# Memory-key reads, residual loads and the last rounds of the down product in a decoder layer on Trainium2

## The chip, the cores and the metric

The kernel runs on one core of one Trainium2 chip. The metric is the device time of one execution in microseconds. The kernel before was timed three times: 1323.92, 1323.97 and 1324.94 us, so its median is 1323.97 us.

## The reference

One layer with three residual sub-layers and a final norm, on 1024 tokens of width 1024, all in fp32. What matters here:

```python
def gla_mixer(...):                     # 4 heads, chunks of 64; per-head norm, gain, gate
    ...
    o = o * lax.rsqrt(jnp.mean(o * o, axis=-1, keepdims=True) + EPS) * gla_gain.astype(f32)
    o = o.reshape(B, T, GLA_VW) * jax.nn.silu(r.astype(f32))

def cross_attn(h, memn, w_q, w_k, w_v, w_o):
    k = (memn @ w_k).reshape(B, MEM_LEN, CROSS_HEADS, CROSS_DH)      # 256 memory tokens
    v = (memn @ w_v).reshape(B, MEM_LEN, CROSS_HEADS, CROSS_DH)
    ...

def conv_ffn(h, w_up, conv_w, conv_b, w_down):                       # D_FF = 2816
    ...
    return (jax.nn.silu(gate) * val) @ w_down

h = x
h = h + jnp.concatenate([o_gla, o_swa], axis=-1) @ w_out[l]
h = h + cross_attn(rms_norm(h, norm_cross[l]), rms_norm(mem, norm_mem[l]), ...)
h = h + conv_ffn(rms_norm(h, norm_ffn[l]), w_up[l], conv_w[l], conv_b[l], w_down[l])
return rms_norm(h, norm_final)
```

`rms_norm(x, g)` is `x * rsqrt(mean(x*x) + EPS) * g` along the row of 1024.

## The kernel before

**Arithmetic.** Every fp32 operand of a large product is split into a high part (a cast on ScalarE, L109) and a low part (a subtraction on VectorE, L110); TensorE then does three matmuls for one product, high by high, high by low and low by high (`mm3`, L148 to L150; in the down stage L1405). Where one engine's queue is spoken of: PE is TensorE, DVE is VectorE, ACT is ScalarE, POOL is GpSimd, SP is SyncE. Instructions run in order on each engine, and a DMA is issued by the engine whose queue it is on.

**Stages.** Input projections; sliding-window attention; gated linear attention (`gla`); the output projection with its residual (`mix_out`); cross attention; the up projection; the down projection (`ffn_down`) with the final norm. The products of the memory tokens with w_v_c (parts 0 to 7) and w_k_c (parts 8 to 15) are strewn into `gla` as filler for TensorE (`memory_parts`). In `gla`, DVE and ACT run in the order in which the code is written; elsewhere a scheduler sets the order from the readiness and the place in the program of each instruction, and "issue after" ties add an order without a semaphore of their own where both stand on one engine.

**Memory keys.** For parts 8 to 15 `multiply(n)` does 24 matmuls of 256 columns into one of two PSUM banks with the role O; `read(n)` takes the bank out: high part on ACT (L362), low part on DVE (L365), then a DMA on the POOL queue to `k_d` (L368). The SBUF target is half of a tile `la`, which two parts share (2 such tiles). A bank is free for `parts(n + 2)` when `read(n)` is done. `gla_scaled` (L921) scales the chunk outputs on ACT, 8 instructions, with the factors of `gla_norm`, which end at L190 on DVE.

**mix_out** has 8 steps of 2 halves, each 24 matmuls of 512 columns; the half's evacuation adds the residual (L1103, DVE) in a tile `res` with 3 buffers. `res` is loaded from `xt_d` on the SP queue (L1078), and written to `h1_d` on the POOL queue (L1081). The weights' split for its first step is tied to come after the transposes that precede it.

**ffn_down** (L1378 ff) multiplies 1024 x 2816 by 2816 x 1024 as 2 x 2 blocks in seven products by Winograd's form of Strassen's rule. Each product has 11 steps k, each of 4 banks, 3 matmuls of 512 columns in each bank: 132 matmuls. Operands of a step are sums of blocks (`comb`, L1391, DVE) or blocks as loaded, and are split into `w` slots: 6 slots are 3 pairs, and pairs are made 2 steps ahead (`AHEAD`). The blocks are summed in place, so the sum b12 - b11 overwrites b11. `snapshot` (L1440) adds a product's banks to the residual; `half_row` (L1445) finishes half a row block and has ACT sum its squares (L196) into `acc`; `gain` (L1450) multiplies by the final norm's gain. `row_factors` gives the rsqrt of the rows' mean squares: the two halves are added (L1458), scaled (L182), Ln and Exp on ACT (L183, L184), and one Newton step of four small DVE operations (L187 to L190). `finish` scales the two halves of a row (ACT L1465, DVE L1468) and issues the output DMAs on the SP and ACT queues. In the seventh product the last 3 steps run bank by bank (`tail=3`), so that banks end one after another; row blocks 0 and 1 share their factors, 2 and 3 have their own.

Of the kernel before, what the change touches and what calls it, by code (L numbers as in the profile page):

```python
# [27 lines left out]
P = 128  # L28
T = 1024
D = 1024  # L30
# [30 lines left out]
class Layer:  # L61
# [282 lines left out]
    def memory_parts(self, new):  # L344
# [42 lines left out]
        def multiply(n):  # L387
# [14 lines left out]
            else:  # L402
# [315 lines left out]
    def gla(self, new, prepare, multiply):  # L718
# [37 lines left out]
        with self.tc.manual_schedule(engines={mybir.EngineType.DVE, mybir.EngineType.Activation}):  # L756
# [63 lines left out]
            newton()  # L820
            o = self.gla_scaled(po, r, new)
            read(13)
# [237 lines left out]
    def mix_out(self, new, hcnew):  # L1060
# [6 lines left out]
        for j in range(NK):  # L1067
# [14 lines left out]
            with self.tc.issue_after(self.turned.ins):  # L1082
# [295 lines left out]
    def ffn_down(self, pre, hcnew):  # L1378
# [9 lines left out]
        acc = self.small("facc", [P, NT, 2], bufs=1)  # L1388

# [9 lines left out]
        def product(ps, left, right, first, before=(), later=(), ops=(), tail=1):  # L1399


# [19 lines left out]
            for k in range(n):  # L1421
# [13 lines left out]
                later = later[cut:]  # L1435

# [15 lines left out]
        def row_factors(t, count):  # L1452

            ssq, r = self.small("fssq", [P, 4])[:, :count], self.small("frs", [P, 4])[:, :count]
            guess, newton = self.rsqrt_steps(r, ssq, D, count)

            def first():
                tt(out=ssq, in0=acc[:, t:t + count, 0], in1=acc[:, t:t + count, 1], op=add)  # L1458
                guess()
            return r, [first, newton]  # L1460

        def finish(t, r, done, dc, todo, tc):

            def f():
                nc.scalar.mul(out=done, in_=done, mul=r)  # L1465
                nc.sync.dma_start(out=self.out[0, t * P:(t + 1) * P, 512 * dc:512 * dc + 512], in_=done)
                sl = slice(512 * tc, 512 * tc + 512)
# [214 lines left out]
```

## Time and profile before

| | us |
|---|---|
| median of 3 runs | 1323.97 |
| profiled execution | 1327.92 |
| its span on the core | 1326.2 |
| TensorE busy | 1304.6 (98% of the span) |
| VectorE busy | 917.9 (69%) |
| ScalarE busy | 588.0 (44%) |
| GpSimd busy | 86.5 (7%) |

The profile is one execution, 3.95 us above the median; 1.72 us of it lie outside the span. TensorE's busy time includes modelled ends of its pipelined matmuls, so consecutive matmuls overlap in the timeline: the distance from one start to the next is what a matmul costs. A timeline row with a count stands for several instructions in a row that are printed together. The bracket behind a row is the idle time of its engine before it, and the instruction whose end came last among those it waited for. A granted clock of 1.00 is TensorE at 2.4 GHz, 0.50 is 1.2 GHz.

### The profile page before, as it was taken

What the parts mean: (1) busy time and instruction counts of PE and PEld (TensorE: products, weight loads), DVE (VectorE), ACT (ScalarE), POOL (GpSimd) and SP (SyncE); (2) the same over time, 40 slices, a digit from 0 to 9 for tenths busy, and PEclk for the clock granted to TensorE, in tenths of its full rate; (3) what the DMA queues carried; (4) which work ended last, traced back from release to release, by engine and by line L of the source; (5) the groups of instructions that cost most, each with busy time, mean ns of one, the idle gap of its engine ahead of it and who ended that gap; (6) DMA issues with size and microseconds to landing.
All of it is one profiled execution on the core that took longest, in us unless ns stands there. A gap on an engine that the chain in (4) does not pass through costs nothing.

```text
span 1326.2 us, 17248 instructions
## 1 busy us (share of the span) xinstructions
PE 1304.6 (98%) x6575; PEld 1081.6 (82%) x6575; DVE 917.9 (69%) x1564; ACT 588.0 (44%) x1041; POOL 86.5 (7%) x150
## 2 busy tenths in 40 slices
PE   8999999999999999999999999999999999999997
PEld 8887777989788888888888888888888888788785
DVE  6939763377444433464469998888888887998766
ACT  6525545345433333463344544443444444454454
POOL 1400111102100000001100000000000000000000
PEclk9999999999999999999999999999999999999998
DMA  7632112259544311143212343222222238710203
GB/s 221 186 110 64 61 56 61 64 169 295 173 158 143 112 64 48 32 167 95 81 56 64 124 137 106 80 96 83 76 81 95 80 109 320 253 64 8 72 21 146
DMA packets 141528, 146.89 MB, mean 111 GB/s; under 512 B 15825, under 2 KB 108166, under 8 KB 141446
## 3 DMA queue, kind: packets, MB, share of 16 engines
q1 hardware_dynamic: 129974, 111.02, 26.9%
q0 software_dynamic: 10304, 32.68, 7.0%
q10 hardware_dynamic: 1168, 2.10, 0.4%
q8 instruction: 51, 0.84, 0.3%
q14 instruction: 31, 0.25, 0.1%
HBM read 109.06 MB, written 38.28 MB: 111 GB/s over the span
## 4 chain that ended last, share of the span: by engine, by line
PE 51%; issue 39%; DVE 4%; DMA 2%; POOL 2%; ACT 1%; SPq 0%; POOLq 0%; DVEq 0%; ACTq 0%
PE psF L148 10%; PE psF L149 9%; PE psF L150 9%; PE psF L1405 4%; PE psS L1405 4%; PE psT L1405 2%; PE psO L1405 2%; PE psO L148 1%; PE psO L149 1%; PE psO L150 1%; DVE w L110 1%; PE psO L1037 1%; PE psS L984 1%; PE psS L1024 1%; POOL g_d L1338 1%
## 5 line engine op out<-in xcount | busy, mean ns | idle before, releaser
L109 ACT CAST w<-st 128x1024 fp32r<-128x1024 f32 (+1 forms) x146 | 125.8, 863 | 276.1 <-PE psF L149 102.7
L110 DVE TENSOR_TENSOR w<-st,w 128x1024 fp32r<-128x1024 f32 (+1 forms) x146 | 144.0, 986 | 74.6 <-ACT w L109 73.9
L1327 DVE SCALAR_TENSOR_TENSOR uy<-uy,vec,uy 128x1023 f32<-128x1023 f32 (+1 forms) x88 | 111.9, 1277 | 0.9 <-ACT uy L1325 0.4
L1405 PE MATMUL psF<-w,w 128*128 128x512 f32 x330 | 93.0, 390 | 0.1
L1405 PE MATMUL psS<-w,w 128*128 128x512 f32 x330 | 92.5, 390 | 0.0
L1298 PE MATMUL psS<-a,w 128*128 128x512 f32 x360 | 86.5, 389 | 0.0
L148 PE MATMUL psF<-xh,w 128*128 128x512 f32 x208 | 83.3, 400 | 0.0
L150 PE MATMUL psF<-xh,w 128*128 128x512 f32 x208 | 81.5, 392 | 0.0
L149 PE MATMUL psF<-xl,w 128*128 128x512 f32 x208 | 81.2, 390 | 0.0
L1298 PEld LDWEIGHTS psS<-a,w 128*128 128x128 f32 x360 | 67.6, 188 | 14.0
L1298 PE MATMUL psF<-a,w 128*128 128x512 f32 x324 | 77.8, 389 | 0.0
L1405 PEld LDWEIGHTS psF<-w,w 128*128 128x128 f32 x330 | 61.8, 188 | 13.9 <-DVE w L110 0.8
L1405 PEld LDWEIGHTS psS<-w,w 128*128 128x128 f32 x330 | 62.0, 188 | 12.9
L1298 PEld LDWEIGHTS psF<-a,w 128*128 128x128 f32 x324 | 60.8, 188 | 12.6
L148 PE MATMUL psF<-act,w 128*128 128x512 f32 x176 | 69.5, 395 | 0.0
L149 PE MATMUL psF<-act,w 128*128 128x512 f32 x176 | 69.1, 392 | 0.0
L150 PE MATMUL psF<-act,w 128*128 128x512 f32 x176 | 68.8, 391 | 0.0
L1325 ACT ACTIVATE uy<-uy,vec 128x1024 f32<-128x1024 f32 x44 | 54.8, 1246 | 24.8 <-DVE uy L1318 16.9
L1298 PE MATMUL psS<-act,w 128*128 128x512 f32 x240 | 57.8, 389 | 0.0
L1298 PE MATMUL psS<-act,wx 128*128 128x512 f32 x240 | 57.6, 389 | 0.0
L1298 PEld LDWEIGHTS psS<-act,wx 128*128 128x128 f32 x240 | 45.1, 188 | 9.3
L1298 PEld LDWEIGHTS psS<-act,w 128*128 128x128 f32 x240 | 45.1, 188 | 9.3
(396 smaller groups left out, 3041.2 us busy)
## 6 DMA issues: line engine op xcount, KB each, us to landing
st<-in_w_up_dram SPq DMA_DIRECT2D x44, 512.0 KB, 4.0
g_d<-uy POOLq DMA_DIRECT2D x22, 512.0 KB, 2.9
act<-in_w_down_dram SPq DMA_DIRECT2D x12, 512.0 KB, 9.9
st<-g_d SPq DMA_DIRECT2D x10, 512.0 KB, 3.9
res<-g_d SPq DMA_DIRECT2D x10, 512.0 KB, 8.7
st<-in_w_in_dram SPq DMA_DIRECT2D x9, 512.0 KB, 6.6
xt_d<-pts POOLq DMA_DIRECT2D x16, 256.0 KB, 5.4
ow_d<-pts POOLq DMA_DIRECT2D x32, 128.0 KB, 3.1
```

What stands on the lines that cost most here:

```text
L109: h = nc.scalar.copy(out=hi, in_=src)
L110: l = nc.vector.tensor_tensor(out=lo, in0=src, in1=hi.bitcast(F32), op=ALU.subtract)
L148: mm(out, lhsT=lh, rhs=rh, start=start, stop=False)
L149: mm(out, lhsT=lh, rhs=rl, start=False, stop=False)
L150: mm(out, lhsT=ll, rhs=rh, start=False, stop=stop)
L984: nc.tensor.matmul(ps[u][g][:, t, :nk], lhsT=self.sq[2 * u + t][pr, q], rhs=self.sk[pr, k0:k0 + nk], start=True, stop=True)
L1024: nc.tensor.transpose(pp[:, 2 * u + t], probs[u][:, 2 * g + t, j * P:(j + 1) * P], self.ident)
L1037: nc.tensor.matmul(po[64 * g:64 * g + 64], lhsT=self.sv[:, k0 // P + j, 64 * g:64 * g + 64], rhs=pts[2 * j + g], start=j == 0, stop=j == n ...
L1298: nc.tensor.matmul(ps, lhsT=b[l][:, q], rhs=a[q][r], start=first and q == 0 and n == 0, stop=first and q == 3 and n == 2, skip_group_check ...
L1325: nc.scalar.activation(out=y, in_=u, func=AF.Identity, scale=self.v("cw2", j), bias=self.v("conv_b", j))
L1327: nc.vector.scalar_tensor_tensor(out=y[:, s:], in0=u[:, :T - s], scalar=self.v(nm, j), in1=y[:, s:], op0=ALU.mult, op1=ALU.add)
L1405: nc.tensor.matmul(ps[i], lhsT=g[:, l, tk], rhs=w[:, r], start=first and k == 0 and m == 0, stop=first and k == n - 1 and m == 2, skip_gro ...
```

## The change

**In `gla` and `memory_parts`.** Parts 8 and 13 get a tile of their own (`lk`, one buffer); the other parts share halves of `la` tiles in the order in which they are made. `read(9)` stands ahead of `parts(10, 11)`, before behind them and the start of the fifth gate. `read(13)` stands ahead of `gla_scaled` of chunk pair 6, before behind it. The weights of `mix_out` are now also tied behind the last of the 8 scalings (`self.scaled`).

**In `mix_out`.** The residual is loaded on the POOL queue, on which its result is written too.

**In `ffn_down`.** `product` returns the low split of each step's second operand; `behind(mark, f, ...)` ties a sum behind such a split without a semaphore. The sums b12 - b11 of product 2's code come behind product 1's last split; the sums of product 3's left operands behind product 2's split of the same step (at least step 2), those of product 7's left operands behind product 6's step 2. Product 6's four half rows of y move from ahead of its steps to between them. The seventh product runs its last four steps bank by bank; its step 10 has operands in tiles `pre` of their own. Row factors work from a part that is known beforehand (`known`: the other half's mean square plus EPS), one fused addition, Ln, Exp, a scaling by -0.5 beside them, and two fused operations for one row block. Each of the rows 0 to 3 has its own factors, and the order of the end on PE, DVE and ACT is as written. Output DMAs of the second halves go out on the POOL queue, that of the last row on the ACT queue.

The diff, cut to its core:

```diff
@@ memory_parts
-                if n % 2 == 0:
-                    keys[:] = [room()]
-                return save(keys[0][:, :, n % 2 * MEM:(n % 2 + 1) * MEM], ps, (k_d[(n - 8) // 2],), n % 2)
+                if n in (8, 13):
+                    t = new("lk", [P, 2, MEM], F32R)
+                else:
+                    if len(keys) == 0:
+                        both = room()
+                        keys[:] = [both[:, :, :MEM], both[:, :, MEM:]]
+                    t = keys.pop(0)
+                return save(t, ps, (k_d[(n - 8) // 2],), n % 2)
@@ gla
             read(8)
+            read(9)
             splits(11)
             gated = self.gla_gated(4, o, new)
             parts(10, 11)
-            read(9)
             splits(12)
...
             newton()
+            read(13)
             o = self.gla_scaled(po, r, new)
-            read(13)
             parts(15)
@@ gla_scaled
-                self.nc.scalar.mul(out=o[p][:, n], in_=po[p][:, n], mul=r[:, 4 * p + n:4 * p + n + 1])
+                self.scaled = self.nc.scalar.mul(out=o[p][:, n], in_=po[p][:, n], mul=r[:, 4 * p + n:4 * p + n + 1])
@@ mix_out
-                nc.sync.dma_start(out=res, in_=self.xt_d[j, :, sl])
+                nc.gpsimd.dma_start(out=res, in_=self.xt_d[j, :, sl])
...
-            with self.tc.issue_after(self.turned.ins):
+            with self.tc.issue_after(self.turned.ins), self.tc.issue_after(self.scaled.ins):
@@ ffn_down
-        def operand(src):
-            t = self.wslot("w", (P, 2, 512))
-            self.split(src, t[:, 0], t[:, 1])
+        def operand(src, new=None):
+            t = new("pre", (P, 2, 512), F32R, 6) if new else self.wslot("w", (P, 2, 512))
+            _, self.low = self.split(src, t[:, 0], t[:, 1])
             return t
+        def behind(mark, f, *args):
+            with self.tc.issue_after(mark.ins):
+                return f(*args)
...
-                    ops.append(tuple(operand(t) for t in srcs[k]))
+                    new = pre if tail > 3 and k == n - 1 else None
+                    ops.append(tuple(operand(t, new) for t in srcs[k]))
+                    lows[k] = self.low
...
+                    if end:
+                        for f in later:
+                            f()
+                        end(lambda i: [step(i, q, *ops[q]) for q in range(n - tail, n)])
+                        break
...
+        def row_factors(t, count, c):
+            stt = nc.vector.scalar_tensor_tensor
+            m, v, y, z, r = (fac[:, x, t:t + count] for x in range(5))
+            def known():
+                nc.vector.tensor_scalar(out=m, in0=acc[:, t:t + count, 1 - c], scalar1=1.0 / D, scalar2=EPS, op0=mult,
+                                        op1=add)
+            def guess():
+                stt(out=v, in0=acc[:, t:t + count, c], scalar=1.0 / D, in1=m, op0=mult, op1=add)
+                nc.scalar.activation(out=z, in_=v, func=AF.Ln)
+                nc.scalar.activation(out=y, in_=z, func=AF.Exp, scale=-0.5)
+                nc.vector.tensor_scalar(out=v, in0=v, scalar1=-0.5, scalar2=None, op0=mult)
+            def newton():
+                if count == 1:
+                    stt(out=m, in0=y, scalar=y, in1=v, op0=mult, op1=mult)
...
+                stt(out=r, in0=m, scalar=1.5, in1=y, op0=add, op1=mult)
...
-        product(y, a12_at, lambda k: b21[k], True,
-                later=[lambda k=k: comb(b11[k], b12[k], b11[k], sub) for k in range(n)] +
-                [snapshot(x[i], c11[i], i, 0) for i in range(4)])
+        lows = product(y, a12_at, lambda k: b21[k], True,
+                                 later=[lambda k=k: behind(lows[n - 1], comb, b11[k], b12[k], b11[k], sub)
+                                        for k in range(n)] + [snapshot(x[i], c11[i], i, 0) for i in range(4)])
         def s1(k):
-            comb(a21[k], a21[k], a22[k], add)
-            comb(a11[k], a21[k], a11[k], sub)
+            mark = lows[max(k, AHEAD)]
+            behind(mark, comb, a21[k], a21[k], a22[k], add)
+            behind(mark, comb, a11[k], a21[k], a11[k], sub)
             return a21[k]
...
-        before += [half_row(y[i], c22[i], 4 + i, 1) for i in range(4)]
-        product(x, lambda k: a22[k], lambda k: b21[k], False, before, [gain(c22[i], 1) for i in range(4)])
+        later = [half_row(y[i], c22[i], 4 + i, 1) for i in range(4)] + [gain(c22[i], 1) for i in range(4)]
+        lows = product(x, lambda k: a22[k], lambda k: b21[k], False, before, later)
...
-            return comb(a12[k], a12[k], a11[k], sub)
+            return behind(lows[AHEAD], comb, a12[k], a12[k], a11[k], sub)
+        def end(bank):
+            with self.tc.manual_schedule(engines={mybir.EngineType.PE, mybir.EngineType.DVE,
+                                                  mybir.EngineType.Activation}):
+                for i in range(4):
+                    bank(i)
...
+                for i in range(4):
+                    half_row(y[i], c12[i], i, 1)()
+                    if i:
+                        rows[i - 1][1]()
+                    _, (_, guess, newton) = factors[i]
+                    guess()
+                    newton()
+                    rows[i][0]()
+                rows[3][1]()
+        product(y, s4, lambda k: b22[k], False, [half_row(x[i], c21[i], 4 + i, 0) for i in range(4)], later, tail=4,
+                end=end)
```

What this does to the order of instructions, at three places. The rows name line, operation, out<-in and shape; line numbers after the change are some lines higher than before.

ScalarE (ACT) near the end of `gla`, before: behind the Ln and Exp of the GLA norm stand the cast of mix_out's first weights (`w<-st`) and the scalings (`o`, 8 in all).

```order
L183 ACTIVATE rs_t_3496<-rs_v_3495 128x8
L184 ACTIVATE rs_y_3497<-rs_t_3496 128x8
L109 CAST w_3597<-st_3593 128x1024
L921 ACTIVATE o_3506<-psF_3396,grs_3494 128x128
L921 ACTIVATE o_3507<-psF_3397,grs_3494 128x128
```

After:

```order
L183 ACTIVATE rs_t_3497<-rs_v_3496 128x8
L184 ACTIVATE rs_y_3498<-rs_t_3497 128x8
L362 CAST lk_3453<-psO_3428 128x256
L926 ACTIVATE o_3510<-psF_3396,grs_3495 128x128
L926 ACTIVATE o_3511<-psF_3397,grs_3495 128x128
```

The cast of part 13's bank (`lk<-psO`, `read(13)`) now stands ahead of the 8 scalings; it stood behind them. The cast of mix_out's weights left its place ahead of them: it now stands behind them and behind the cast of part 14's bank.

VectorE (DVE) in product 1 of the down stage, before: `pre` and `act` hold blocks of a and b, `uy` belongs to the last of the up stage; L1391 are sums, L110 splits.

```order
L1391 TENSOR_TENSOR pre_9215<-act_9287,pre_9215 128x512
L1337 TENSOR_TENSOR uy_9248<-uy_9248,uy_9252 128x1024
L110 TENSOR_TENSOR w_9342<-pre_9217,w_9342 128x512
L110 TENSOR_TENSOR w_9345<-pre_9219,w_9345 128x512
L110 TENSOR_TENSOR w_9360<-pre_9221,w_9360 128x512
L110 TENSOR_TENSOR w_9363<-pre_9223,w_9363 128x512
L110 TENSOR_TENSOR w_9378<-pre_9221,w_9378 128x512
L110 TENSOR_TENSOR w_9381<-pre_9223,w_9381 128x512
L1391 TENSOR_TENSOR pre_9215<-act_9287,pre_9215 128x512
L1391 TENSOR_TENSOR pre_9219<-act_9289,pre_9219 128x512
```

After:

```order
L1342 TENSOR_TENSOR uy_9250<-uy_9250,uy_9254 128x1024
L110 TENSOR_TENSOR w_9344<-pre_9219,w_9344 128x512
L110 TENSOR_TENSOR w_9347<-pre_9221,w_9347 128x512
L110 TENSOR_TENSOR w_9362<-pre_9223,w_9362 128x512
L110 TENSOR_TENSOR w_9365<-pre_9225,w_9365 128x512
L110 TENSOR_TENSOR w_9380<-pre_9223,w_9380 128x512
L110 TENSOR_TENSOR w_9383<-pre_9225,w_9383 128x512
L110 TENSOR_TENSOR w_9398<-act_9227,w_9398 128x512
L110 TENSOR_TENSOR w_9401<-act_9229,w_9401 128x512
L110 TENSOR_TENSOR w_9416<-act_9227,w_9416 128x512
```

The sum ahead of the up stage's last operation and the sums behind product 1's splits of steps 3 to 5 have gone behind its last split.

DVE from product 5 to product 6, before: `st` are tiles of product 7's left operand (sums L1391), L1440 the four snapshots of product 5, L1445 the half rows.

```order
L1391 TENSOR_TENSOR st_10691<-st_10691,pre_9221 128x512 x2
L110 TENSOR_TENSOR w_10487<-res_9500,w_10487 128x512
L1440 TENSOR_TENSOR act_9287<-psT_9300,act_9287 128x512
L1440 TENSOR_TENSOR act_9287<-psO_9301,act_9287 128x512
L1440 TENSOR_TENSOR act_9289<-psF_9302,act_9289 128x512
L1440 TENSOR_TENSOR act_9289<-psS_9303,act_9289 128x512
L1445 TENSOR_TENSOR act_9287<-psF_9757,act_9287 128x512
L1445 TENSOR_TENSOR act_9287<-psS_9758,act_9287 128x512
L1445 TENSOR_TENSOR act_9289<-psF_9759,act_9289 128x512
L1445 TENSOR_TENSOR act_9289<-psS_9760,act_9289 128x512
L110 TENSOR_TENSOR w_10490<-act_9272,w_10490 128x512
```

After (L1461 is the snapshot, L1466 the half row):

```order
L110 TENSOR_TENSOR w_10470<-act_9274,w_10470 128x512
L110 TENSOR_TENSOR w_10477<-res_9502,w_10477 128x512
L1461 TENSOR_TENSOR act_9289<-psT_9302,act_9289 128x512
L1461 TENSOR_TENSOR act_9289<-psO_9303,act_9289 128x512
L1461 TENSOR_TENSOR act_9291<-psF_9304,act_9291 128x512
L1461 TENSOR_TENSOR act_9291<-psS_9305,act_9291 128x512
L110 TENSOR_TENSOR w_10480<-act_9274,w_10480 128x512
L110 TENSOR_TENSOR w_10495<-res_9506,w_10495 128x512
L110 TENSOR_TENSOR w_10498<-act_9276,w_10498 128x512
L1466 TENSOR_TENSOR act_9289<-psF_9759,act_9289 128x512
```

The sums of product 7 and three of the four half rows have left this place; the splits of product 6's steps 1 and 2 follow the snapshots, and a first half row comes behind them.

On the queues, the 16 residual loads of mix_out move from SP to POOL. There they stand as: three loads, two writes of results, two loads, and from then on a write and a load in turn; each load into a buffer that was written out follows that write on the queue.

## Rows read from the trace of the kernel before

**Rows 1.** Part 1 of the page: busy time of TensorE, share of the span, instructions.

```profile
PE 1304.6 (98%) x6575; PEld 1081.6 (82%) x6575; DVE 917.9 (69%) x1564; ACT 588.0 (44%) x1041; POOL 86.5 (7%) x150
```

**Rows 2.** The view of waits for TensorE, whole span. Columns: engine, tile and line that waits, what it waited for, total us, times, longest us.

```profile
PE psO L148 <- DVE la L365: 3.5, 2, 2.9
...
PE psT L1405 <- DVE w L110: 1.8, 3, 0.8
```

**Rows 3.** The timeline of the end of the GLA stage, 334 to 345 us. Columns here and in the other timelines: start us, us, engine, line, operation, out<-in, shape, count, and in brackets the idle time before it and what ended that.

```profile
334.69 0.17 DVE L190 TENSOR_TENSOR grs<-rs_y,rs_t 128x8 f32<-128x8 f32 x1
...
335.73 1.05 ACT L109 CAST w<-st 128x1024 fp32r<-128x1024 f32 x1 [2.23 <-DMA st<-in_w_out_dram]
...
336.69 2.16 ACT L921 ACTIVATE o<-psF,grs 128x128 f32<-128x128 f32 x8
...
336.81 1.23 DVE L110 TENSOR_TENSOR w<-st,w 128x1024 fp32r<-128x1024 f32 x1 [1.96 <-ACT w L109]
...
339.14 0.76 DVE L365 TENSOR_TENSOR la<-psO,la 128x256 fp32r<-128x256 f32 x2 [1.10 <-ACT la L362]
...
339.62 0.58 PE L148 MATMUL psO<-wg,w 128*128 128x256 f32 x1 [2.92 <-DVE la L365]
...
344.01 1.03 PE L933 MATMUL psS<-ident,o 128*128 128x128 f32 x8
```

**Rows 4.** The view of windows over the same stretch. Columns: window, its length, busy us and count of PE, PEld, DVE, ACT and POOL, granted TensorE clock, DMA share, GB/s.

```profile
339.50:342.50 3.00, 2.88 (x13) 2.88 (x14) 1.62 (x3) 0.83 (x1) 1.39 (x2) 0.50 0.91 269
...
343.00:344.00 1.00, 1.00 (x10) 1.00 (x10) 0.00 (x0) 0.00 (x0) 0.00 (x0) 1.00 0.81 238
```

**Rows 5.** The timeline of one step of the memory keys earlier in the GLA stage, 321 to 325 us.

```profile
322.06 0.38 PE L148 MATMUL psO<-wg,w 128*128 128x256 f32 x1 [0.59 <-DVE la L365]
...
324.26 0.41 DVE L365 TENSOR_TENSOR la<-psO,la 128x256 fp32r<-128x256 f32 x1
```

**Rows 6.** The timeline of the start of mix_out, 349 to 357 us (an SPq or POOL row is the time its queue took to issue, waits included).

```profile
349.39 0.67 POOL L368 DMA_DIRECT2D k_d<-la  x1 [8.04 <-DVE la L365]
...
352.86 6.45 SPq L1078 DMA_DIRECT2D res<-xt_d  x4
...
356.29 0.50 PE L148 MATMUL psF<-x,w 128*128 128x512 f32 x1 [0.33 <-DVE res L1103]
```

**Rows 7.** The view of DMAs of the mix_out stage, 352 to 440 us. Columns: transfer, queue, count, KB each, median us from issue to landing.

```profile
res<-xt_d SPq DMA_DIRECT2D x16, 256.0 KB, 3.1
h_d<-res POOLq DMA_DIRECT2D x16, 256.0 KB, 2.4
```

**Rows 8.** The view of windows over products 1, 3, 4, 5 and 6 of the down stage, each from its first matmul to the next product's first (columns as in the other view of windows).

```profile
1102.53:1134.38 31.85, 30.81 (x133) 24.55 (x132) 27.32 (x41) 14.91 (x23) 0.53 (x1) 1.00 0.87 318
...
1164.36:1194.67 30.31, 30.24 (x133) 24.68 (x132) 29.35 (x49) 15.54 (x32) 0.00 (x0) 1.00 0.20 70
...
1194.67:1224.60 29.93, 29.93 (x134) 24.79 (x133) 24.35 (x40) 12.57 (x22) 0.00 (x0) 1.00 0.03 9
...
1224.60:1255.32 30.72, 30.08 (x133) 24.62 (x132) 22.59 (x38) 13.18 (x24) 0.00 (x0) 1.00 0.25 78
...
1255.32:1286.21 30.89, 30.11 (x132) 24.60 (x132) 21.36 (x35) 14.84 (x31) 0.00 (x0) 1.00 0.01 1
```

**Rows 9.** The timeline of product 1 of the down stage.

```profile
1108.55 0.69 DVE L1391 TENSOR_TENSOR pre<-act,pre 128x512 f32<-128x512 f32 x1 [0.63 <-DMA act<-in_w_down_dram]
...
1110.29 3.09 DVE L110 TENSOR_TENSOR w<-pre,w 128x512 fp32r<-128x512 f32 x5
...
1111.63 0.73 PE L1405 MATMUL psT<-w,w 128*128 128x512 f32 x2 [0.55 <-DVE w L110]
...
1125.59 0.69 DVE L1391 TENSOR_TENSOR res<-res,res 128x512 f32<-128x512 f32 x1 [3.74 <-DMA res<-g_d]
...
1128.74 0.74 PE L1405 MATMUL psT<-w,w 128*128 128x512 f32 x2 [0.49 <-DVE w L110]
```

**Rows 10.** The timeline from product 5 to product 6.

```profile
1252.67 1.30 DVE L1391 TENSOR_TENSOR st<-st,pre 128x512 f32<-128x512 f32 x2 [0.81 <-DMA st<-g_d]
...
1254.49 0.69 DVE L1440 TENSOR_TENSOR act<-psT,act 128x512 f32<-128x512 f32 x1
...
1255.32 0.93 PE L1405 MATMUL psT<-w,w 128*128 128x512 f32 x3 [0.65 <-ACT w L109]
...
1258.68 0.68 DVE L1445 TENSOR_TENSOR act<-psS,act 128x512 f32<-128x512 f32 x1
...
1260.01 0.73 PE L1405 MATMUL psT<-w,w 128*128 128x512 f32 x2 [0.78 <-DVE w L110]
```

**Rows 11.** The timeline of the end of the kernel.

```profile
1314.63 2.20 PE L1405 MATMUL psS<-w,w 128*128 128x512 f32 x9
...
1316.22 1.41 DVE L1468 SCALAR_TENSOR_TENSOR c<-c,frs,nfin 128x512 f32<-128x512 f32 x2
...
1317.62 0.68 DVE L1445 TENSOR_TENSOR c<-psS,c 128x512 f32<-128x512 f32 x1
...
1319.24 0.16 DVE L1458 TENSOR_TENSOR fssq<-facc 128x1 f32<-128x1 f32 x1 [0.88 <-ACT junk L196]
...
1320.17 0.74 DVE L1468 SCALAR_TENSOR_TENSOR c<-c,frs,nfin 128x512 f32<-128x512 f32 x1
...
1321.40 0.75 DVE L1468 SCALAR_TENSOR_TENSOR c<-c,frs,nfin 128x512 f32<-128x512 f32 x1
```

More of the change, by code (lines that the diff above doesn't have):

```diff
@@ L1388, in ffn_down @@
         acc = self.small("facc", [P, NT, 2], bufs=1)
+        fac = self.small("ffac", [P, 5, NT], bufs=1)
         def comb(out, x, y, op):
@@ L1392, in comb, with product @@
             return out
-        def operand(src):
-            t = self.wslot("w", (P, 2, 512))
-            self.split(src, t[:, 0], t[:, 1])
-            return t
-        def product(ps, left, right, first, before=(), later=(), ops=(), tail=1):
+        def operand(src, new=None):
+            t = new("pre", (P, 2, 512), F32R, 6) if new else self.wslot("w", (P, 2, 512))
+            _, self.low = self.split(src, t[:, 0], t[:, 1])
+            return t
+        def behind(mark, f, *args):
+            with self.tc.issue_after(mark.ins):
+                return f(*args)
+        def product(ps, left, right, first, before=(), later=(), ops=(), tail=1, end=None):
+            lows = {}
             def step(i, k, g, w):
@@ L1435, in product @@
                 later = later[cut:]
+            return lows
         def snapshot(ps, dst, t, c):
@@ L1450, in gain, with finish, one, two @@
             return lambda: tt(out=dst, in0=dst, in1=nfin[:, 512 * c:512 * c + 512], op=mult)
[L1452 to L1464, printed above, removed]
+        def row_factors(t, count, c):
[12 more added lines that the diff above has]
+                    stt(out=m, in0=y, scalar=y, in1=v, op0=mult, op1=mult)
+                else:
+                    tt(out=m, in0=y, in1=y, op=mult)
+                    tt(out=m, in0=m, in1=v, op=mult)
+                stt(out=r, in0=m, scalar=1.5, in1=y, op0=add, op1=mult)
+            return r, [known, guess, newton]
+        def finish(t, r, done, dc, todo, tc, queue=nc.gpsimd):
+            def one():
                 nc.scalar.mul(out=done, in_=done, mul=r)
                 nc.sync.dma_start(out=self.out[0, t * P:(t + 1) * P, 512 * dc:512 * dc + 512], in_=done)
+            def two():
                 sl = slice(512 * tc, 512 * tc + 512)
                 nc.vector.scalar_tensor_tensor(out=todo, in0=todo, scalar=r, in1=nfin[:, sl], op0=mult, op1=mult)
-                nc.scalar.dma_start(out=self.out[0, t * P:(t + 1) * P, sl], in_=todo)
-            return f
+                queue.dma_start(out=self.out[0, t * P:(t + 1) * P, sl], in_=todo)
+            return one, two
         def take(gen, count):
@@ L1499, in ffn_down @@
         c12 = [self.dnew("c12", [P, 512], F32, 4) for _ in range(4)]
-        product(x, lambda k: a11[k], lambda k: b11[k], True, ops=ops)
+        lows = product(x, lambda k: a11[k], lambda k: b11[k], True, ops=ops)
         blocks((a, (1, 0)), (a, (1, 1)))
@@ L1556, in s4 @@
                 take(a12s, 1)
-            return comb(a12[k], a12[k], a11[k], sub)
-        r, steps = row_factors(4, 4)
-        product(y, s4, lambda k: b22[k], False, [half_row(x[i], c21[i], 4 + i, 0) for i in range(4)],
-                steps + [finish(4 + i, r[:, i:i + 1], c22[i], 1, c21[i], 0) for i in range(4)], tail=3)
-        for i in range(2):
-            half_row(y[i], c12[i], i, 1)()
-        r, (first, newton) = row_factors(0, 2)
-        first()
-        half_row(y[2], c12[2], 2, 1)()
-        newton()
-        for i in range(2):
-            finish(i, r[:, i:i + 1], c11[i], 0, c12[i], 1)()
-        r, (first, newton) = row_factors(2, 1)
-        first()
-        half_row(y[3], c12[3], 3, 1)()
-        newton()
-        finish(2, r, c11[2], 0, c12[2], 1)()
-        r, steps = row_factors(3, 1)
-        for f in steps:
-            f()
-        finish(3, r, c11[3], 0, c12[3], 1)()
+            return behind(lows[AHEAD], comb, a12[k], a12[k], a11[k], sub)
+        r, steps = row_factors(4, 4, 0)
+        factors = [row_factors(i, 1, 1) for i in range(4)]
+        later = steps + [f for i in range(4) for f in finish(4 + i, r[:, i:i + 1], c22[i], 1, c21[i], 0)]
+        later += [known for _, (known, _, _) in factors]
+        def end(bank):
[3 more added lines that the diff above has]
+                    bank(i)
+                rows = [finish(i, factors[i][0], c11[i], 0, c12[i], 1, nc.scalar if i == 3 else nc.gpsimd)
+                        for i in range(4)]
+                for i in range(4):
[9 more added lines that the diff above has]
+                end=end)
     def run(self):
```

3 lines of the change are left out of this document (removed).

## The prediction

> **What bounds the kernel now.** I read the page's busy times first: TensorE works for 98% of the span [rows 1], so only the places where it waits or runs at half clock can give time. The view of waits for TensorE names them [rows 2]: two waits for a memory-key bank (3.5 us, one of 2.9) and three short ones in the down stage for an operand's low split. From there I went to the timeline at each place, to see what the awaited engine did just before, and to the windows, since a stretch can lose more than its listed wait. For the down stage I compared each product's length with the shortest: product 4 takes 29.93 us for 132 matmuls, 0.2267 us each [rows 8], which I take as the undisturbed cost. The end of the kernel, behind the last matmul, I read as a chain of its own.
>
> **End of the GLA stage.** Part 15's matmuls wait 2.92 us, until 339.62, for the low half of part 13's bank [rows 3]. Before that read, ACT casts mix_out's weights (335.73, 1.05 us) and does eight scalings (336.69, 2.16 us), although the factors were there at 334.69 + 0.17. After the wait the granted clock is 0.50 until about 342.5, then 1.00 [rows 4]: TensorE, idle for 2.92 us, restarts on the lower level (1.2 GHz) and the 24 matmuls take 344.01 - 339.62 = 4.39 us. In the clocked-down window 13 matmuls take 3.0 us (0.23 each), in the fast one 10 take 1.0; at a price between half of 0.23 and 0.10 the 24 would take 2.4 to 2.8 us; I take 2.8. After the change the bank is read ahead of the scalings, which start at about 334.9 and end at 337.1; the low half (about 0.4 us, half of the pair at 339.14 [rows 3]) follows the Newton step on DVE at about 335, over 1 us ahead of 336.7, when part 15 wants its bank. So part 15 ends at 336.7 + 2.8 = 339.5 in place of 344.01, **4.5 to 4.6 us** gained if the work behind it is ready. What is late next: mix_out's first weights, now cast behind the scalings and part 14's cast: 337.1 + 0.4 (taken like the low half) + 1.05 = 338.55, plus the subtraction of 1.23 [rows 3] and hand-overs: 339.9. The eight transposes behind part 15 (about 0.8 us) cover TensorE until 340.2. The margin is 0.3 us. I take 4.6; ends 3.0 (wait gone, weights late by 1.5) and 5.0.
>
> **Earlier key read.** The wait of 0.59 us at 322.06 [rows 5] is for part 9's bank, read behind a later split and the gate. Read earlier, it vanishes; but part 12 then wants part 10's bank, which DVE, no less loaded here, read at 324.26. 0 to 0.6; I take **0.3**.
>
> **Residual loads.** The SP queue took the first loads at 352.86, behind the landing of the last key write (issued 349.39), and TensorE waited 0.33 us for the first residual sum [rows 6]. On POOL the loads stand behind that write's issue, which comes 4.6 us earlier. Gain **0.3** (0 to 0.35). POOL takes about 0.6 us for an issue and is idle for most of the stage; what the move could cost is a rival, below.
>
> **Product 1** takes 31.85 us, 1.92 over product 4 [rows 8]. Two stops are seen [rows 9]. At 1111.63 TensorE resumes after a split that began at 1110.29, since DVE first did a sum that had waited 0.63 us for its DMA (1108.55), and then the up stage's last product. At 1128.74 it resumes after a split behind sums, the first of which had waited 3.74 us for a DMA. DVE runs in order, so a sum that isn't urgent but waits for a transfer holds up an urgent split. With the sums tied behind product 1's last split neither can happen; the up stage's last operation can then start about 0.6 us earlier and the split at 1109.2 to 1109.8, before TensorE wants it (1110.9). Gain **1.9** (1.0 to 1.95). The tied sums aren't gone: 11 of them, at 0.60 us from start to start (five in 3.09 with the last one's 0.69 [rows 9]), make 6.6 us of DVE work that moves into products 2 and 3, a rival below. The left sums of product 3, tied behind the splits of product 2, can no longer go ahead of those: product 3 has lost 30.31 - 29.93 = 0.38 [rows 8]; gain **0.35** (-0.5 to 0.4).
>
> **Products 5 and 6** are 0.79 and 0.96 over product 4 [rows 8]. Between them TensorE waits until 1255.32, since product 5's snapshot (1254.49) is behind two sums for product 7, which had waited 0.81 us for a load [rows 10]. It waits again until 1260.01, since four half rows (the last at 1258.68) precede the split of step 1. Now the sums are tied behind product 6's third split and the half rows come between the steps; the order above shows the splits directly behind the snapshots. Gain **1.75** (1.2 to 1.8). What is late next is only the first split of product 6, made ahead of the snapshots as before.
>
> **The end.** Before: the last matmul ends at 1314.63 + 2.20 = 1316.83; the fourth half row could start then, but DVE is in two row products (1316.22, 1.41 us) and starts it at 1317.62; its squares are there for 1319.24, 1.62 later; then the factor takes 2.16 us to 1321.40, 0.6 of them behind another row product at 1320.17 [rows 11]. After: four steps bank by bank instead of three, so each bank ends 12 matmuls, 2.72 us, after the one before. DVE has time for row 2 before bank 3 ends, so the fourth half row starts 0.1 after it. Against that, bank 0 wants the operands of four steps within 2.72 us: before, the three-step tail took 0.3 us more than its 36 matmuls, and I expect 0.6 now, so the last matmul ends at 1317.1. Then 1317.2 + 1.6 = 1318.8 for the squares, and for the factor five small steps at about 0.2 each (the small addition at 1319.24 takes 0.16): 1.0 in place of 2.16. The last row product starts at 1319.8 in place of 1321.40: **1.6** (0.6 to 2.2). The last DMA follows on ACT's queue as before.
>
> **Sum**: 4.6 + 0.3 + 0.3 + 1.9 + 0.35 + 1.75 + 1.6 = 10.8 us. The profiled run of 1327.92 (span 1326.2) would become about 1317.1 (1315.4 of span). It was 3.95 above the median, and none of the places above is likely to hold that difference, so I take the sum from the median: 1323.97 - 10.8 = 1313.2.
>
> **Rivals.**
> *Weights late or clock not in play.* If mix_out's weights are 1.5 us late, TensorE waits there, perhaps on the lower clock again; or if the unprofiled runs don't lose the 1.6 us to the clock. Against the first stand 0.3 us of margin, small enough to count. 1313.2 + 1.5 to 2.5: about 1315.
>
> *DVE becomes the bound in products 2 and 3.* DVE is busy 29.35 of 30.31 us in product 3 [rows 8], and 6.6 us of sums are added behind product 1. For: no gap there before. Against: before, it ran ahead of its need, and product 4 left it 5.6 us idle. Counted along the new order at 0.60 us for a 512-column operation, each split is still ready 0.4 to 2 us ahead of its matmul. If not, up to 3 us: 1316.
>
> *The ties do little.* The stop in product 1 was the wait for a late load, and an operand load that is late itself stops the split as well; and the end's four-step tail could starve. Without the gain in product 1 and at the end, 3.5 less: 1316.7.
>
> *The POOL queue holds the residual up: slower.* TensorE gives a half of mix_out 24 x 0.2267 = 5.44 us. On POOL each load into a used buffer stands right behind the write from that buffer and must wait for its landing, and the next write stands behind that load. One turn is then an issue (about 0.55), the write's landing and another issue. Now writes land after 2.4 us and loads after 3.1 [rows 7], so the turn is about 3.5, under 5.44. It decides from a landing of 4.3 us on; above, each of 13 turns falls behind by the excess, with some 7.5 us of lead used up first. At a landing of 6.1 the turn is 7.2: 13 x 1.76 - 7.5 = 15.4 us lost, 1328.6. For it: DVE is busy beside the queue, and the queue has had writes alone until now. The Trainium skill (SBUF — State Buffer, "Who interferes with whom") says that a DMA that seems stalled by VectorE is one whose descriptors GpSimd writes, and that it should go to a hardware queue; this speaks against the move. Writes on the POOL queue land no later than the SP queue's loads in these rows [rows 7], so the trace bears little of it out.
>
> **How the numbers follow.** Forecast 1313.2, chance 0.72, its own range 1311.4 to 1315. Weights or clock 0.10, DVE as the bound 0.07, ties of little effect 0.06, POOL queue 0.05. The range reaches to 1316.8 to take in most of the three middle cases, and down to 1311.4, just under the sum of the terms' upper ends (12.3 gained, 1311.7). A measurement of this kernel can tell about 0.2%, 2.65 us, from no change: faster is under 1321.3. All but the last case lie there; I leave 0.03 for several of them at once or a part of the last. Faster 0.93, same 0.03, slower 0.04.
>
> **What would show it right or wrong.** Right: the waits for TensorE list neither the bank of part 13 nor the split waits of the down stage; the granted clock stays 1.00 from 336 to 346; mix_out starts 4.6 us earlier, less or more 0.3; products 1, 3, 5 and 6 take 29.9 to 30.2 us each; from the last matmul's end to the last row product it is 2.7 us in place of 4.6. Wrong: a wait for the weights' split at mix_out's start; a wait of TensorE for L1103's sum, with POOL's loads spaced by more than 5.44 us; a product 2 or 3 longer than before with splits behind sums; a tail that loses over 1 us within its 48 matmuls.

## The result and the profile after

The changed kernel takes 1328.0 us (median of 16 runs), the kernel before 1324.58 us beside it (16 runs). The ratio is 1.0025, 95% interval 1.0019 to 1.0032: slower by a quarter of a per cent, against a forecast of 0.8% faster. One of the 16 runs, at 1867 us, ran at a mean granted clock of 0.655 and is left out of the ratio.

The odd thing is that nearly everything forecast was there. The view of waits for TensorE of the changed kernel:

```profile
PE psO L250 <- DMA vrows<-in_norm_mix_dram: 3.2, 1, 3.2
PE psS L511 <- DMA gr<-in_x_dram: 1.2, 1, 1.2
PE psF L148 <- ACT w L112: 0.6, 1, 0.6
PE psS L989 <- DVE mx L998: 0.4, 1, 0.4
PE psO L148 <- DVE la L365: 0.4, 1, 0.4
PE psF L1418 <- DVE w L110: 0.3, 1, 0.3
```

Against [rows 2], the bank wait of 2.9 us and the three split waits of the down stage (1.8 us) are gone; what is left is 0.4 us of part 12's wait for the bank of part 10, and one split wait of 0.3 us in the tail of the seventh product. At the end of the GLA stage the timeline of the changed kernel has part 13's cast first, then the scalings, then the weights, as planned:

```profile
333.06 0.37 ACT L362 CAST lk<-psO 128x256 fp32r<-128x256 f32 x1 [0.39 <-PE psO L150]
...
334.07 2.17 ACT L926 ACTIVATE o<-psF,grs 128x128 f32<-128x128 f32 x8 [0.64 <-DVE grs L190]
...
336.33 2.07 ACT L109 CAST w<-st 128x1024 fp32r<-128x1024 f32 x2
...
338.52 1.03 PE L938 MATMUL psS<-ident,o 128*128 128x128 f32 x8
```

The transposes start at 338.52, 5.5 us earlier than before [rows 3]. The view of windows over products 1 to 6, each from its first matmul to the next one's:

```profile
1107.82:1137.76 29.94, 29.94 (x134) 24.77 (x132) 22.55 (x33) 14.91 (x23) 0.53 (x1) 1.00 0.92 326
1137.76:1167.68 29.92, 29.92 (x134) 24.77 (x132) 29.92 (x51) 13.95 (x25) 0.00 (x0) 1.00 0.56 204
1167.68:1197.60 29.92, 29.92 (x134) 24.77 (x132) 29.92 (x51) 15.86 (x32) 0.00 (x0) 1.00 0.18 62
1197.60:1227.52 29.92, 29.92 (x134) 24.77 (x132) 28.23 (x51) 12.58 (x22) 0.00 (x0) 1.00 0.03 9
1227.52:1257.44 29.92, 29.92 (x134) 24.77 (x132) 19.42 (x33) 12.57 (x22) 0.00 (x0) 1.00 0.25 80
1257.44:1287.36 29.92, 29.92 (x134) 24.77 (x132) 24.62 (x43) 15.70 (x31) 0.00 (x0) 1.00 0.01 2
```

Every product takes the 29.9 us that product 4 took before [rows 8]; DVE is busy all through products 2 and 3 (29.92 of 29.92 us) and still holds nothing up. And the end of the changed kernel:

```profile
1317.50 0.85 PE L1418 MATMUL psS<-pre,pre 128*128 128x512 f32 x3
...
1318.39 0.69 DVE L1466 TENSOR_TENSOR c<-psS,c 128x512 f32<-128x512 f32 x1 [0.16 <-PE psS L1418]
...
1319.87 0.16 DVE L1484 SCALAR_TENSOR_TENSOR ffac<-facc,ffac 128x1 f32<-128x1 f32 x1
...
1321.01 0.75 DVE L1506 SCALAR_TENSOR_TENSOR c<-c,ffac,nfin 128x512 f32<-128x512 f32 x1
```

The last matmul ends at 1318.35, the last row product starts 2.66 us later; it was 1321.40 - 1316.83 = 4.57 before [rows 11], and the forecast was 2.7.

But look at the starts: the down stage begins at 1107.82, and before at 1102.53 [rows 8]. A lead of 5.5 us at 338, 5.7 at the end of mix_out, has become a lag of 5.3 at 1107, in cross attention and the up projection, which the change does not touch. The windows from 690 to 1100 us, of the kernel before:

```profile
690.00:1100.00 410.00, 410.00 (x1810) 339.62 (x1809) 351.48 (x413) 181.67 (x208) 11.25 (x21) 1.00 0.30 97
```

and of the changed kernel:

```profile
690.00:1100.00 410.00, 410.00 (x1772) 332.43 (x1771) 348.20 (x406) 180.65 (x205) 11.26 (x21) 1.00 0.29 92
```

Both are 100% busy at a granted clock of 1.00, and the changed kernel does 38 matmuls fewer in the same time. The page cannot show this as a wait: it shows as a busier TensorE, 1311.7 us in place of 1304.6 [rows 1]:

```profile
PE 1311.7 (99%) x6575; PEld 1080.6 (82%) x6575; DVE 919.5 (69%) x1566; ACT 590.5 (45%) x1043; POOL 99.1 (7%) x173
```

The view by tile says which matmuls; its columns are duration minimum, median and maximum in ns, and first and last start. The kernel before, 820 to 1080 us, matmuls on the tile `act`:

```profile
L1298 PE MATMUL psS<-act,wx x168: 388/389/390, 819.6 to 1056.1; 128*128 128x512 f32 x168
L1298 PE MATMUL psS<-act,w x168: 388/389/390, 827.8 to 1064.2; 128*128 128x512 f32 x168
```

and the changed one:

```profile
L1303 PE MATMUL psS<-act,w x168: 395/396/397, 827.3 to 1068.7; 128*128 128x512 f32 x168
L1303 PE MATMUL psF<-act,wx x168: 395/396/397, 838.4 to 1079.8; 128*128 128x512 f32 x168
```

Every matmul that reads `act` takes 7 ns longer. In the starts of the same matmuls, the 912 of the up projection, that is 0.2335 us from one to the next in place of 0.2267. With those of cross attention there are 1584 on `act`, and their starts add up to 9.9 us more than before. Of the 684 matmuls on `a`, the first five behind each group on `act` are slower too, which makes 0.2287 on average: 684 x 0.002 = 1.4. Together that is 11.3 us, and the whole stretch from mix_out's end to the down stage's start is 11.0 us longer (680.92 in place of 669.95). In mix_out and in the down stage the spacing is 0.2267 in both kernels.

What moved `act`? The small tiles. `ffac` takes 160 bytes per partition, and `fssq` and `frs`, which it replaces, took 192 (six buffers of 32). All later tiles on that side of SBUF start 32 bytes lower; `act` starts at 12224 in place of 12256. The kernel has a filler of 296 words named `shift` ahead of `act`, in `run`, which does no work; the diff does not touch it.

### The profile page after: what moved, and what is told of

It is laid out like the page before. It is cut to its first block, busy times and chain, and to the rows that moved or that the text cites. A ratio compares the mean times of both kernels' runs of the same rounds, so it can differ in the third digit from the quotient of the medians.

```text
span 1325.6 us, 17250 instructions
## 1 busy us (share of the span) xinstructions
PE 1311.7 (99%) x6575; PEld 1080.6 (82%) x6575; DVE 919.5 (69%) x1566; ACT 590.5 (45%) x1043; POOL 99.1 (7%) x173
## 4 chain that ended last, share of the span: by engine, by line
PE 94%; issue 3%; DVE 1%; DMA 1%; POOL 1%; ACT 0%; SPq 0%; POOLq 0%; DVEq 0%; ACTq 0%
PE psS L1303 15%; PE psF L1303 13%; PE psF L148 12%; PE psF L149 12%; PE psF L150 12%; PE psS L1418 6%; PE psF L1418 6%; PE psT L1418 2%; PE psO L1418 2%; PE psS L148 2%; PE psS L150 1%; PE psS L149 1%; PE psO L148 1%; PE psO L149 1%; PE psO L150 1%
## 5 line engine op out<-in xcount | busy, mean ns | idle before, releaser
L110 DVE TENSOR_TENSOR w<-st,w 128x1024 fp32r<-128x1024 f32 (+1 forms) x145 | 143.9, 993 | 73.3 <-ACT w L109 58.5
L1303 PEld LDWEIGHTS psS<-act,w 128*128 128x128 f32 x240 | 45.1, 188 | 10.8
```

The source lines that it names most:

```text
L110: l = nc.vector.tensor_tensor(out=lo, in0=src, in1=hi.bitcast(F32), op=ALU.subtract)
L1303: nc.tensor.matmul(ps, lhsT=b[l][:, q], rhs=a[q][r], start=first and q == 0 and n == 0, stop=first and q == 3 and n == 2, skip_group_check ...
```

## The experiments

Theory: the matmuls on `act` became slower because `act` moved against the weights. Rivals: another part of the change (POOL traffic, the new order) slows them; or a start address is slow by itself.

**Run 1, the changed kernel with `act` where it was.**

```diff
-            hcs.enter_context(self.pool("shift"))("shift", [P, 296])
+            hcs.enter_context(self.pool("shift"))("shift", [P, 304])
```

> The changed kernel, with the filler tile ahead of the act tiles 32 bytes larger, so that act and all later tiles of that side start where they do in the kernel before. In the changed kernel each matmul whose moving operand is an act tile takes 0.233 us, 0.2267 before; from 432 to 1102 us this costs 10.9 us. Theory A (the act tiles' start address, 32 bytes lower since the small tiles shrank by that much): 0.2267 again, 1328.0 - 10.9 = 1317 us. Rival B (the slower matmuls come from another part of the change, such as traffic on the POOL queue): no change, 1328.

Measured 1317.11 us, before 1324.97: ratio 0.994 (0.9927 to 0.9952). Its matmuls on `act` are back at the duration before:

```profile
L1303 PE MATMUL psS<-act,w x168: 389/389/389, 823.6 to 1060.0; 128*128 128x512 f32 x168
L1303 PE MATMUL psF<-act,wx x168: 389/389/389, 834.5 to 1070.9; 128*128 128x512 f32 x168
```

Eight words of an unused tile are worth 10.9 us, the whole of the loss, and the rest of the change is a gain.

**Run 2, the kernel before with `act` 32 bytes lower** (`shift` of 288 words), nothing of the change in it.

> The kernel before, with that filler 32 bytes smaller and nothing else: act starts at 0 modulo 64, as in the changed kernel, the weights stay at 32. Theory A: act matmuls 0.233 us, 10.9 us slower than before, about 1335.5 us. Rival B: as before, 1324.6.

1335.15 us, ratio 1.0077 (1.0064 to 1.009). The loss comes without the change: rival B falls.

**Runs 3 and 4, the other side moved too.** A tile of 32 bytes ahead of the weights' pool puts everything on that side 32 bytes lower; `shift` is 288 words in the first and 280 in the second.

```diff
+        wstack.enter_context(self.pool("wshift", "right"))("wshift", [P, 8])
         self.wnew = wstack.enter_context(self.pool("wpool", "right"))
```

> The kernel before, all tiles of both sides 32 bytes lower: act, the weights and every other large operand at 0 modulo 64. If the moving operand's own start decides (A1: 0 modulo 64 is slow): act, a, x, q, xh and w matmuls all at 0.233, some 4500 x 0.0067 = 30 us slower, about 1355. If the moving and the stationary operand must start alike modulo 64 (A2): as before, 1324.6.

> The kernel before, act and its side 64 bytes lower (32 modulo 64 as before), the weights and the other side 32 lower (0 modulo 64). A1: act at 0.2267, the rest (x, q, a, w, xh) at 0.233, some 19 us slower, about 1343. A2: act at 0.233, the rest at 0.2267, about 1335.5.

With both sides 32 lower: 1323.75, ratio 0.9992 (0.9983 to 1.0002), no loss. With `act` 64 and the rest 32 lower: 1334.69, ratio 1.0075 (1.0061 to 1.0089). The tile view of the first has 389 ns again:

```profile
L1298 PE MATMUL psS<-act,w x168: 389/389/389, 824.7 to 1061.1; 128*128 128x512 f32 x168
```

That of the second has 396:

```profile
L1298 PE MATMUL psS<-act,wx x168: 395/396/397, 821.6 to 1063.0; 128*128 128x512 f32 x168
L1298 PE MATMUL psS<-act,w x168: 395/396/397, 829.9 to 1071.3; 128*128 128x512 f32 x168
```

So it isn't an address as such; the distance between the two sides decides.

**Runs 5 to 9, which distance.** The kernel before with `shift` 64, 128, 256, 512 and 1024 bytes smaller.

> The kernel before with the filler 64 bytes smaller: act starts at 32 modulo 64 as the weights do, but at 32 modulo 128 where the weights are at 96. If offsets modulo 64 must agree: as before, 1324.8. If it is modulo 128: act matmuls at 0.233 us, about 1335.5.

> The kernel before with the filler 128 bytes smaller: act and the weights agree modulo 128, no more modulo 256. If agreement modulo 128 is enough: act matmuls at 0.2267, as before, about 1325. If more is needed: 0.233 and about 1335.

> The kernel before with the filler 256 bytes smaller. If act and the weights must agree modulo 256 or less than that: act matmuls at 0.2267 us, about 1325. If modulo more: 0.233, about 1335.

> The same, 512 bytes smaller. Agreement modulo 512 enough: 0.2267 us, about 1325; if not, 0.233, about 1335.

> The same, 1024 bytes smaller. Agreement modulo 1024 enough: 0.2267 us, about 1325; if only modulo 2048: 0.233, about 1335.

| kernel | act | w | distance modulo 256 | us per matmul on act, up projection | us |
|---|---|---|---|---|---|
| before | 12256 | 110560 | 0 | 0.2267 | 1324.6 |
| changed | 12224 | 110560 | 32 | 0.2335 | 1328.0 |
| changed, `act` moved back | 12256 | 110560 | 0 | 0.2267 | 1317.1 |
| before, 32 lower | 12224 | 110560 | 32 | 0.2335 | 1335.2 |
| before, both 32 lower | 12224 | 110528 | 0 | 0.2267 | 1323.8 |
| before, 64 and 32 lower | 12192 | 110528 | 32 | 0.2335 | 1334.7 |
| before, 64 lower | 12192 | 110560 | 64 | 0.2333 | 1334.7 |
| before, 128 lower | 12128 | 110560 | 128 | 0.2328 | 1334.3 |
| before, 256 lower | 12000 | 110560 | 0 | 0.2267 | 1323.3 |
| before, 512 lower | 11744 | 110560 | 0 | 0.2267 | 1324.1 |
| before, 1024 lower | 11232 | 110560 | 0 | 0.2267 | 1322.9 |

(Addresses are the first buffers' starts in bytes per partition, as the built programs have them; the spacing is the mean from one start to the next of the 912 matmuls on `act` in the up projection, from the traces. The last three times are of one run each.) My first guess, that agreement modulo 64 would do, failed with the distance of 64, and modulo 128 with 128. A distance of a multiple of 256 bytes is enough, and every other one tried (32, 64, 128) costs 0.006 to 0.007 us per matmul. A tile view at a distance of 128:

```profile
L1298 PE MATMUL psS<-act,wx x168: 387/394/399, 824.8 to 1065.4; 128*128 128x512 f32 x168
```

**Runs 10 to 14, what the parts bring**, each the aligned change of run 1 with one part undone. Loads of the residual back on SP:

```diff
-                nc.gpsimd.dma_start(out=res, in_=self.xt_d[j, :, sl])
+                nc.sync.dma_start(out=res, in_=self.xt_d[j, :, sl])
```

> The changed kernel with the filler of the first run (1317.1 us), and mix_out's residual loads back on the SP queue. The prediction has the move to POOL as a gain of 0.3: 1317.4. In the trace of the first run TensorE waits 1.2 us for the first residual sum, 0.3 to 0.7 in traces of the kernel before: if the move costs, 1316.5.

1316.55 us, ratio 0.9931 (0.9918 to 0.9945): no difference to run 1 that the intervals show.

The sums without ties:

```diff
         def behind(mark, f, *args):
-            with self.tc.issue_after(mark.ins):
-                return f(*args)
+            return f(*args)
```

> The changed kernel with the filler of the first run, and the sums of the down product without their ties to operand splits. If the ties bring what the prediction says (1.9 in product 1, 0.35 in product 3, half of 1.75 in products 5 and 6): 1317.1 + 3.1 = 1320.2. From the traces of the first run and the third (kernel before, all at 0), product by product: 1.3 + 0.4 + 0.7, 1319.5. Rival, the ties do little since a late load was the cause: 1317.1.

1318.45 us, ratio 0.9947 (0.9934 to 0.9961), 1.3 above run 1. Product 1 of this kernel:

```profile
1096.43:1128.05 31.62, 30.84 (x134) 24.55 (x133) 27.35 (x41) 14.91 (x23) 0.53 (x1) 1.00 0.91 330
```

31.62 in place of 29.92 us: the stops are back, so the ties made them go. By the starts in the trace products 3, 5 and 6 take 30.35, 30.08 and 30.02: in all 1.7 + 0.4 + 0.3 = 2.4 us for the ties, of which the times show 1.3. Run 1 and this one were on different occasions, and the difference lies within the two intervals; beside the run with the loads on SP, of its own occasion, it is 1.9.

The GLA part undone:

```diff
             newton()
-            read(13)
             o = self.gla_scaled(po, r, new)
+            read(13)
...
-            with self.tc.issue_after(self.turned.ins), self.tc.issue_after(self.scaled.ins):
+            with self.tc.issue_after(self.turned.ins):
```

(and `read(9)` and the tiles of the keys as before.)

> The changed kernel with the filler of the first run, and the GLA part undone (bank reads 9 and 13 at their old places, key tiles in pairs, mix_out's weights cast ahead of the scalings). By the prediction 4.9 us slower: 1322.0. By the traces of the first and the third run, in which part 15 waits 1.1 us and the clock does not fall: 2.2 slower, 1319.3.

1319.74 us, ratio 0.9954 (0.9941 to 0.9968): 2.6 above run 1, and 3.2 above the run with the loads on SP, of its own occasion, where the prediction had 4.9.

Product 6's half rows early:

```diff
-        later = [half_row(y[i], c22[i], 4 + i, 1) for i in range(4)] + [gain(c22[i], 1) for i in range(4)]
+        before += [half_row(y[i], c22[i], 4 + i, 1) for i in range(4)]
+        later = [gain(c22[i], 1) for i in range(4)]
```

> The changed kernel with the filler of the first run, and product 6's four half rows ahead of its steps as before the change. By the prediction the second stop (0.96 us in product 6) returns: 1317.1 + 1.0 = 1318.1. Rival: without the sums ahead of them the snapshots are done sooner and the splits have time: 1317.1.

1317.36 us, ratio 0.9945 (0.9932 to 0.9957). In its trace the split of product 6's second step is late again, and TensorE stops as in [rows 10]:

```profile
1250.31 0.68 DVE L110 TENSOR_TENSOR w<-act,w 128x512 fp32r<-128x512 f32 x1
...
1251.04 0.72 PE L1418 MATMUL psT<-w,w 128*128 128x512 f32 x2 [0.48 <-DVE w L110]
```

Product 6 takes 30.71 us, 0.79 more; the time shows 0.25, less than the runs can tell. The old end (last three steps bank by bank, the old row factors and queues; `fssq` and `frs` are back, so `shift` stays at 296):

> The changed kernel with the end of the kernel before (three steps bank by bank, its row factors and output queues); the small tiles are then as before, so act lies as before without a larger filler. By the prediction 1.6 us slower than the first run: 1318.7; by the traces of the first and third run 1.9: 1319.0. Rival, the end is bound by the output DMAs and gains nothing: 1317.1.

1319.14 us, ratio 0.9959 (0.9945 to 0.9972): 2.0 above run 1.

**Runs 15 to 17, three steps at the end, and both small things together.** `tail=3` in place of 4; then that and the loads on SP, beside run 1 once more on the same chip.

> The changed kernel with the filler of the first run, and three steps bank by bank at the end in place of four, all else of the end kept. In the first run's trace the four-step tail loses 0.7 us against its matmuls. If that is all that counts: 1316.5. If banks that end 2.04 us apart in place of 2.72 leave DVE behind (half row 0.69, row product 0.75, small steps): 1317.1 to 1317.8.

> The kernel of the first run again (the change with act moved back), for comparison on the same chip: 1317.1.

> The same with the residual loads on the SP queue and three steps bank by bank. If POOL costs 0.6 and the fourth step 0.1, as single runs had it: 1316.4. If both were spread between chips: 1317.1. By the prediction (POOL a gain of 0.3): 1317.4.

1317.06 us, ratio 0.9944 (0.9932 to 0.9957) with `tail=3`; 1317.24, ratio 0.9945 (0.9932 to 0.9959) for run 1 again; 1318.29, ratio 0.9952 (0.994 to 0.9965) with both edits. What single comparisons had as 0.6 and 0.1 us in their favour is not there on one chip: neither the queue nor the fourth step shows a gain or a loss beyond the intervals. The aligned change, at 1317.1 to 1317.2, is the version that beats both kernels, and none of the variants is shown to beat it.

## Why the prediction was wrong

The step that failed stands in its first paragraph: "only the places where it waits or runs at half clock can give time". From it I took the cost of a matmul, 0.2267 us, as given for the whole kernel, and looked for losses only in waits. The change replaces two small tags by one of another size, and I costed what its operations do, never where they lie. That moved `act` by 32 bytes against the weights and took back 10.9 us, more than the gain. None of my rivals was of this kind. The slower side was right in sign only, and by another mechanism: the POOL queue holds nothing up that the times show.

The terms themselves, without the shift:

| term | forecast | measured | from |
|---|---|---|---|
| end of GLA and earlier read | 4.6 + 0.3 | 2.6 | GLA part undone |
| residual loads | 0.3 | nothing that shows | loads on SP, and both edits on one chip |
| product 1 | 1.9 | 1.7; 0.7 to 1.5 | trace without ties; eight experiments' traces of the kernel before |
| product 3 | 0.35 | 0.4 | trace without ties |
| products 5 and 6 | 1.75 | 1.9 | kernel before, both sides 32 lower: 30.58 and 31.14 |
| the end | 1.6 | 2.0 | old end |
| sum | 10.8 | 7.9 and 7.2 in all | 1324.97 - 1317.11, 1324.42 - 1317.24 |

The rows mix times and single traces: with 1.7 for product 1 they add up to 8.6, more than the 7.2 to 7.9 that the change brings in all.

The term of quite another size is the end of GLA, and its cause is the profiled run. In [rows 3] the weights' cast had waited 2.23 us for its load, so the scalings behind it started only at 336.69; TensorE then waited 2.92 us and restarted on the lower clock [rows 4]. In the trace of the kernel before with both sides 32 bytes lower the cast found its weights in time:

```profile
333.61 1.05 ACT L109 CAST w<-st 128x1024 fp32r<-128x1024 f32 x1 [0.32 <-PE psO L149]
334.69 2.18 ACT L921 ACTIVATE o<-psF,grs 128x128 f32<-128x128 f32 x8
```

and TensorE resumes with a short wait and on the full clock:

```profile
337.64 0.38 PE L148 MATMUL psO<-wg,w 128*128 128x256 f32 x1 [1.07 <-DVE la L365]
```

In the nine experiments' traces with the old order of this place, this one among them, the wait was 1.07 to 1.96 us, and the granted clock fell to 0.50 in one of them, the one with 1.96. So the profiled run was the slow end of a spread. How often the timed runs reach it is not shown; of 43 timed runs of the kernel before, two had its mean granted clock of 0.996, the others 0.997 or 0.998. I saw that it was 3.95 us above the median, and wrote that none of the places was likely to hold the difference. This place held most of it: mix_out starts at 344.81 there, and at 341.40 with both sides 32 bytes lower. Product 1 was an extreme too: its 31.85 us are the longest in any of the traces, and in the eight of the experiments on the kernel before it took 30.63 to 31.45. That the clock might not be in play was among my rivals, at 0.10; it deserved more.

The rest went by its steps. The waits were removed where the order said so, the 6.6 us of sums that moved into products 2 and 3 made DVE busy to 100% there without a late split, and the end gained its 2 us; how much of that is the row factors and how much the new order was not taken apart. The early key read can't be told from the spread: from part 8's first matmul to part 14's it is 21.41 us in run 1, 21.76 with the GLA part undone, and 21.04 to 22.47 in the traces of the kernel before; its time was measured only together with the end of GLA.

The residual term was wrong in kind: TensorE's wait for the first residual sum was 0.3 to 0.7 us in traces with the loads on SP, and between nothing and 1.5 with them on POOL, so the move makes it vary and brings no steady gain.

## What to carry to other kernels

When a change adds, drops or resizes any tile, compare the start addresses of the large matmul operands before and after: a saving of 32 bytes in small tiles cost more here than all the removed waits gained. A filler tile in front of an operand may be doing work, and has to be set anew when anything allocated ahead of it changes. And take the size of a wait from several executions when the profiled one lies above the median by more than the term is worth.

## What the runs showed of the hardware

In an unbroken row, a 512-column matmul of this kernel takes 0.2267 us when the start of its moving operand and that of the weights lie a multiple of 256 bytes apart in the partition, and 0.2328 to 0.2335 us at distances of 32, 64 and 128 (the 912 on `act` in the up projection), at a granted clock of 1.00 in all of them.

Behind a break, be it other shapes or a row of operands at another distance, the first five or so take 0.228 to 0.236 us even at a distance of 0; those on `a` behind `act` are a case of it. In the trace with both sides moved, `w` and `wg` are at a distance of 0. A row of them behind matmuls of 128 columns runs like this, from its second one on:

```profile
272.84 0.39 PE L149 MATMUL psO<-w,wg 128*128 128x512 f32 x1
273.07 0.40 PE L150 MATMUL psO<-w,wg 128*128 128x512 f32 x1
273.31 0.39 PE L148 MATMUL psO<-w,wg 128*128 128x512 f32 x1
273.54 0.40 PE L149 MATMUL psO<-w,wg 128*128 128x512 f32 x1
273.77 0.39 PE L150 MATMUL psO<-w,wg 128*128 128x512 f32 x1
274.00 0.39 PE L148 MATMUL psO<-w,wg 128*128 128x512 f32 x1
```

From the last of these on it is 0.227 each; at the distance of 32 in the kernel before it never gets there. Neighbours count too: at the end of the changed kernel the threes on `pre`, both operands of which agree but lie 32 bytes off the `w` around them, took 0.233 us on average, and 0.228 in run 1, where all agree.

That it is the stationary operand, and not another tile on that side, is argued and not shown by itself. A second pair speaks for it. The 96 matmuls of `w` and `wg` in the GLA stage, where the moving operand is the one on the weights' side, took 0.234 us (median) at a distance of 32 modulo 256 (before), 0.229 at 64 (changed) and 0.227 at 0 (both sides moved). In the kernel before, `act` is at 0 and fast and this pair at 32 and slow; with `act` 64 and the rest 32 lower it is the other way round. At 64 this pair loses only a third of what `act` loses, so the distance alone does not set the size. The 192 matmuls of 256 columns with `wg` moving don't follow it (medians of 0.118, 0.118 and 0.120 us at the same three). Why the chip does this stays open.
